# A first attention block's queries prepared among the last gates, and one ring of five tiles for two kinds of filler

## The chip, the cores and the metric

One core of one Trainium2 chip runs the whole program in one launch. The time is device microseconds of one execution; the kernel before took 1732.0 us, the median of three runs (1731.62 to 1733.96). A core has five engines with a queue each: TensorE (PE, matmuls and transposes), VectorE (DVE), ScalarE (ACT), GpSimd (POOL) and SyncE (SP), which here issues the DMAs. Each engine takes its instructions in a fixed order; a waiting instruction holds all that stand behind it.

## The reference

One inference step of a hybrid encoder on 1088 tokens (1024 of a prompt, 64 of a sample with 128 cached keys). Cut to what matters here:

```python
h = rmsnorm(x); p = h @ w_in          # columns of three branches and three gate blocks
qa, ka, va, qi, ki, wi, ub, qm, gates = split(p)
# branch A: per query, an indexer picks the best 256 admissible keys, then attention
score = einsum('bths,bth->bts', relu(einsum('bthd,bsd->bths', qi, ki)), wi)
_, sel = top_k(where(adm, score, -inf), topk)
out_a = softmax(q . k_sel) @ v_sel     # 8 query heads, 2 key heads, head_dim 64
# branch B: trailing means over 2, 4, 8, 16 frames, a linear map per group
# branch M: cross-attention into 256 memory tokens
merged = sum_b sigmoid(gate_b) * (branch_b @ w_o_b)
x += merged @ w_out; x += swiglu(rmsnorm(x))
```

The outputs are the new x and the new cache entries. Every product is made in float32 accuracy from values split into a high and a low part in a rounded format: three matmuls (high by high, low by high, high by low) for one.

## The kernel before

The tokens lie in nine blocks of 128 (the last has 64). The work goes in stages: projections of the branches; selection of the keys by a bisection on DVE and ACT (L835 to L893: counts of scores above a step, then a new step); attention over block after block with the unselected keys masked; output projection and the feed-forward part. While DVE and ACT are bound by the bisection, PE is given filler: the gates (`fill_gate`, L603, tiles named fsg, a tanh on ACT at L243, then a store), the products of the pooling branch (`fill_ob`, L609, tiles named fpt), and inside the attention the products of the memory branch (`fill_om`, L629, tiles named gt). Gates and products go through DRAM: a gate tile is stored; `fill_ob` loads a stored gate tile (L616), DVE multiplies it with the product (L619), and the result is stored into side_m (L620); `fill_om` loads two tiles of side_m (L626), DVE multiplies (L638), POOL adds (L639), and the sum is stored into side_a (L640). All three take their sums from the PSUM tile fl.

In the program's text 48 gate tiles come first, then 24 pooling tiles, later 24 more gate tiles. The gate tiles have a ring of two, the pooling tiles a ring of three: the load into a slot waits for the store out of it.

The attention goes over the blocks in the order 2, 0, 1, 3, 8, 4, 5, 6, 7. For each, `queries_t` (L928) loads the queries (q), splits them (ACT L936, DVE L937, tile qs), transposes eight heads on PE (L940) and copies the result on ACT (L942, tile qT). `softmax` makes the logits on PE (L961, PSUM tile tr), adds the mask and takes the extreme value on DVE (L965, mx), the exponential on ACT (L967), and the division on POOL (L969 a power, L971 a scaling). `values` transposes the probabilities (L984), splits them (ACT L987, DVE) and multiplies by the values (L991).

On POOL and DVE, in the stretch from 440 to 545 us, the head normalisation of projected rows also runs: POOL makes a reciprocal root (L125 a scaling, L126 a power, tile hr), DVE applies it (L216, tile qn) and rotates (L152 to L155) with the tables cosa and sina, which POOL scales after their load (L546, L547). L893 on DVE moves the scores by a rank in the bisection.

The order on each engine is not the program's text. The whole is traced in a context with a scheduler (`schedule_with_timeline_sim=True`) that plays the instructions through a simulated time and lets the one that is ready go; so a change at one place can alter the order on every engine around it.

Of the kernel before, what the change touches and what calls it, by code (L numbers as in the profile page):

```python
# [8 lines left out]
F32 = mybir.dt.float32  # L9
F32R = mybir.dt.float32r  # L10
AF = mybir.ActivationFunctionType
OP = mybir.AluOpType
# [17 lines left out]
HA, HDA = 8, 64  # L30
# [3 lines left out]
NP = NF // 2  # L34
NEG = -1e30
FPT, FSG = 3, 2
ACT_SEL = (3, 5, 7)
DVE_SEL = (8, 2, 4, 6)
INADM = -3.0e38
# [6 lines left out]
def encoder_step(ctx: ExitStack, tc: tile.TileContext, a: dict, o: list):  # L46
# [30 lines left out]
    def mm(dt=F32):  # L77
        return psum[0].tile([128, 512], dt, name="mm", tag="mm", bufs=n_mm[0])
# [126 lines left out]
    def raw_tile():  # L205
        return wp.tile([128, 1024], F32, name="raw", tag="raw", bufs=3)
# [32 lines left out]
    def fsig(w, c0, cn, low_last=False):  # L239
        ps = fps(cn)  # L240
        gate_block(w, hh[:, :, c0:c0 + cn], hl[:, :, c0:c0 + cn], ps, low_last)
        sg = fil.tile([128, 384], F32, name="fsg", tag="fsg", bufs=FSG)[:, :cn]
        A.activation(sg, ps, AF.Tanh, scale=0.5)  # L243
        return sg

# [4 lines left out]
    with tc.tile_pool(name="xphase", bufs=1) as xp:  # L250
# [11 lines left out]
        for c in (0, 512):  # L262
            ps = mm()
# [345 lines left out]
    def fill_ob():  # L609
        for f in range(KT):  # L610
            if f % 2 == 0:
                ow = wblock(a["w_ob"][f:f + 2].rearrange("f p k j -> p f k j"), (2, 4, 128), fraw())
            for c0, cn in CH:
                c1 = c0 + cn
                pt = fil.tile([128, 384], F32, name="fpt", tag="fpt", bufs=3)[:, :cn]
                SP.dma_start(pt, gate_b[f, :, c0:c1])  # L616
                ps = fps(cn)
                matmul3(ps, [(ow[0][:, f % 2, k], ow[1][:, f % 2, k], bh[:, k, c0:c1], bl[:, k, c0:c1]) for k in range(4)])
                V.scalar_tensor_tensor(pt, pt, 1.0, ps, op0=OP.add, op1=OP.mult)  # L619
                SP.dma_start(side_m[f, 1, :, c0:c1], pt)  # L620
# [177 lines left out]
    load_keys(0, 384)  # L798


    for b in range(2):
        V.memset(score[b], 0.0)
        V.memset(score[b][0:64, nkey[b] - 64:], -NEG)
# [109 lines left out]
    with tc.tile_pool(name="att", bufs=1, side="right") as ap_:  # L913
# [12 lines left out]
                lo_of(vb[:n, b0:b1, kv, 1], vs, vb[:n, b0:b1, kv, 0])  # L926

        def queries_t(b):  # L928
            t0, n = TS[b]
            q = ap_.tile([128, HA, HDA], F32, name="q", tag="q", bufs=2)  # L930
            ld = SP.dma_start(q[:n].rearrange("p h d -> p (h d)"), q_a[t0:t0 + n])
            if b in KEYS_AT:
                with tc.issue_after(ld.ins):
                    load_keys(*KEYS_AT[b])
            qs = ap_.tile([128, HA, 2, HDA], F32R, name="qs", tag="qs", bufs=1)
            A.copy(qs[:n, :, 0], q[:n])  # L936
            V.tensor_tensor(qs[:n, :, 1], q[:n], qs[:n, :, 0].bitcast(F32), op=OP.subtract)  # L937
            ps = tr(F32R)
            for h in range(HA):
                PE.transpose(ps[:, h * 128:h * 128 + n], qs[:n, h].rearrange("p s d -> p (s d)"), ident_r[:n, :n])  # L940
            qT = ap_.tile([128, HA, 128], F32R, name="qT", tag="qT", bufs=2)
            A.copy(qT[:, :, :n], ps.rearrange("p (h t) -> p h t", h=HA)[:, :, :n])  # L942
            return qT
# [64 lines left out]
                fill_om(*rest.pop(0))  # L1008
                n -= 1

        for b in (2,0,1,3,8,4,5,6,7):
            qT = queries_t(b)
            for kv in range(2):
                probs = softmax(b, kv, qT)
                if todo:
                    fill(todo[0] // 3 if todo[0] < 8 else 2)
                    values(*todo)
                todo = (b, kv, probs)
                fill(-1, 1)
        values(*todo)  # L1020
    kv2_c.__exit__(None, None, None)
    kv_c.__exit__(None, None, None)
    sel_c.__exit__(None, None, None)
    ps2_c.__exit__(None, None, None)
# [511 lines left out]
```

## Time and profile before

| | |
|---|---|
| median of three runs | 1732.0 us (1731.62 to 1733.96) |
| the profiled execution, its time | 1732.96 us |
| the profiled execution, its span | 1731.1 us |
| PE, DVE, ACT, POOL busy | 1692.6, 1172.7, 809.2, 418.6 us |
| mean granted clock of PE | 0.996 of full speed |

The span goes from the first to the last instruction, the time of an execution includes what lies around it. Busy times of the engines overlap. A granted clock of 1.00 is the full clock of PE; 0.5 would be half of it.

### The profile page before, as it was taken

What the parts mean: (1) busy time and instruction counts of PE and PEld (TensorE: products, weight loads), DVE (VectorE), ACT (ScalarE), POOL (GpSimd) and SP (SyncE); (2) the same over time, 40 slices, a digit from 0 to 9 for tenths busy, and PEclk for the clock granted to TensorE, in tenths of its full rate; (3) what the DMA queues carried; (4) which work ended last, traced back from release to release, by engine and by line L of the source; (5) the groups of instructions that cost most, each with busy time, mean ns of one, the idle gap of its engine ahead of it and who ended that gap; (6) DMA issues with size and microseconds to landing.
All of it is one profiled execution on the core that took longest, in us unless ns stands there. A gap on an engine that the chain in (4) does not pass through costs nothing.

```text
span 1731.1 us, 32521 instructions
## 1 busy us (share of the span) xinstructions
PE 1692.6 (98%) x12088; PEld 1640.9 (95%) x12088; DVE 1172.7 (68%) x2602; ACT 809.2 (47%) x1951; POOL 418.6 (24%) x474
## 2 busy tenths in 40 slices
PE   8999999999999999999899999999999999999999
PEld 7999999999899998877798999999999999999999
DVE  7566999999964443788874688656668556475553
ACT  5457577746532442569732344334334333353431
POOL 4201325355421122775302442001101000000000
PEclk9999999999999999999999999999999999999999
DMA  7121541233366325750273327442535443497761
GB/s 235 56 68 57 174 143 47 73 98 98 109 198 205 100 93 170 244 181 1 78 264 115 113 92 242 150 150 99 203 135 182 150 150 122 144 344 257 213 191 52
DMA packets 147262, 250.85 MB, mean 145 GB/s; under 512 B 16920, under 2 KB 93328, under 8 KB 147104
## 3 DMA queue, kind: packets, MB, share of 16 engines
q1 hardware_dynamic: 147104, 248.78, 43.8%
q8 instruction: 95, 1.56, 0.4%
q14 instruction: 63, 0.52, 0.1%
HBM read 173.63 MB, written 75.09 MB: 144 GB/s over the span
## 4 chain that ended last, share of the span: by engine, by line
PE 77%; DVE 9%; ACT 5%; issue 4%; DMA 3%; POOL 2%; SPq 0%; DVEq 0%; ACTq 0%; POOLq 0%
PE mm L1190 24%; PE mm L122 19%; PE fl L122 14%; PE mm L1417 13%; ACT junk_a L835 2%; PE acc L991 1%; DVE junk_v L838 1%; PE tr L961 1%; DVE wlo L86 1%; PE mm L984 1%; PE mm L379 1%; DVE pl L86 1%; DVE lo L86 1%; DMA side_m<-fpt 1%; DMA gt<-side_m 1%
## 5 line engine op out<-in xcount | busy, mean ns | idle before, releaser
L1190 PE MATMUL mm<-hi,whi 128*128 128x288 f32 (+1 forms) x1120 | 323.0, 289 | 2.3 <-ACT whi L1182 2.3
L1190 PE MATMUL mm<-hi,wlo 128*128 128x288 f32 (+1 forms) x1120 | 323.4, 290 | 0.1
L1190 PE MATMUL mm<-lo,whi 128*128 128x288 f32 (+1 forms) x1120 | 323.4, 289 | 0.0
L1190 PEld LDWEIGHTS mm<-hi,whi 128*128 128x128 f32 x1120 | 211.8, 189 | 3.0 <-ACT whi L1182 3.0
L1190 PEld LDWEIGHTS mm<-lo,whi 128*128 128x128 f32 x1120 | 211.7, 189 | 0.0
L1190 PEld LDWEIGHTS mm<-hi,wlo 128*128 128x128 f32 x1120 | 211.0, 189 | 0.4 <-DVE wlo L86 0.4
L122 PE MATMUL fl<-hh,whi 128*128 128x362 f32 (+1 forms) x576 | 189.9, 330 | 1.7 <-DVE fpt L619 1.0
L122 PE MATMUL fl<-hl,whi 128*128 128x362 f32 (+1 forms) x576 | 189.5, 329 | 0.1
L122 PE MATMUL fl<-hh,wlo 128*128 128x362 f32 (+1 forms) x576 | 188.0, 330 | 0.0
L1417 PE MATMUL mm<-ul,wh 128*128 128x256 f32 (+1 forms) x600 | 171.7, 288 | 0.0
L1417 PE MATMUL mm<-uh,wh 128*128 128x256 f32 (+1 forms) x600 | 171.2, 288 | 0.0
L1417 PE MATMUL mm<-uh,wl 128*128 128x256 f32 (+1 forms) x600 | 170.3, 288 | 0.0
L86 DVE TENSOR_TENSOR wlo<-raw,whi 128x1024 fp32r<-128x1024 f32 (+1 forms) x76 | 77.1, 1026 | 58.7 <-ACT whi L1182 38.6
L835 ACT ACTIVATE junk_a<-score,cand_a,sgn_a 128x512 f16<-128x512 f32 (+2 forms) x93 | 95.5, 1027 | 43.5 <-DVE cand_a L852 31.2
L1417 PEld LDWEIGHTS mm<-ul,wh 128*128 128x128 f32 x600 | 112.7, 188 | 0.0
L1417 PEld LDWEIGHTS mm<-uh,wh 128*128 128x128 f32 x600 | 112.4, 188 | 0.0
L1417 PEld LDWEIGHTS mm<-uh,wl 128*128 128x128 f32 x600 | 112.2, 188 | 0.0
L122 PEld LDWEIGHTS fl<-hh,whi 128*128 128x128 f32 x576 | 108.1, 188 | 3.0 <-POOL whi L96 1.2
L122 PEld LDWEIGHTS fl<-hl,whi 128*128 128x128 f32 x576 | 108.2, 188 | 0.9 <-DVE hl L86 0.4
L122 PEld LDWEIGHTS fl<-hh,wlo 128*128 128x128 f32 x576 | 108.0, 188 | 0.6
L86 DVE TENSOR_TENSOR wl<-raw,wh 128x512 fp32r<-128x512 f32 x75 | 51.7, 690 | 69.8 <-ACT wh L1407 69.8
L838 DVE TENSOR_SCALAR_CACHE_REDUCE junk_v<-score,cand_v 64x192 f16<-64x192 f32 (+1 forms) x124 | 93.9, 757 | 2.6
(410 smaller groups left out, 4669.7 us busy)
## 6 DMA issues: line engine op xcount, KB each, us to landing
uf<-u SPq DMA_DIRECT2D x75, 272.0 KB, 4.7
raw<-in_w_up_dram SPq DMA_DIRECT2D x26, 512.0 KB, 4.3
fraw<-in_w_gates_dram SPq DMA_DIRECT2D x23, 512.0 KB, 3.9
fr<-in_w_gate_dram SPq DMA_DIRECT2D x22, 512.0 KB, 4.3
dr<-in_w_down_dram SPq DMA_DIRECT2D x22, 512.0 KB, 5.7
s<-dr SPq DMA_DIRECT2D x22, 512.0 KB, 3.1
raw<-s SPq DMA_DIRECT2D x44, 256.0 KB, 3.8
side<-side_a SPq DMA_DIRECT2D x8, 1088.0 KB, 6.1
```

Of the source, the lines that this page charges most:

```text
L86: return V.tensor_tensor(lo, src, hi.bitcast(F32), op=OP.subtract)
L122: PE.matmul(ps, l, r, start=i == 0, stop=i == len(prods) - 1)
L379: PE.matmul(ps[:n, :cn], qt[:, h, :n], kstack[:, k0 + c:k0 + c + cn], start=True, stop=True)
L835: A.activation(junk[:n, :nk], sc, AF.Sign, bias=bj, scale=1.0 if scale is None else scale[:n, j:j + 1], accum_out=sj)
L838: V.tensor_scalar(junk[:n, :nk], sc, bj, None, op0=OP.is_ge, op1=OP.add, accum_out=sj)
L961: PE.matmul(lg[:n, i * 512:i * 512 + cn], qT[:, h, :n], kT[:, kv, s, k0 + c:k0 + c + cn], start=s == 0, stop=s == 1)
L984: PE.transpose(pt[:cn, i * n:(i + 1) * n], probs[i][:, c:c + cn], ident[:n, :n])
L991: PE.matmul(acc, vv, r, start=ji == 0 and i == 0, stop=ji == nj - 1 and i == 1)
L1190: PE.matmul(dst[i], l, r, start=start and j == 0, stop=stop and j == 11, skip_group_check=True)
L1417: PE.matmul(acc[f, i], l[:, fs], r[:, cs], start=start and j == 0, stop=stop and j == 2, skip_group_check=True)
```

## The change

The first block of the attention (block 2) has its queries loaded into a borrowed weight tile (`raw`), split and transposed right behind the first load of keys, in the program's text before attention's pools are opened and so, for the scheduler, free to run beside the last gates. The split is made a function that both places call. The transposes use two PSUM tiles of 512 columns (mm) in place of one of 1024 (tr), so the copy on ACT is in two halves, and the result lies in a small pool of its own that stays open to the end of the attention. Gate tiles and pooling tiles take one ring of five.

```diff
-        sg = fil.tile([128, 384], F32, name="fsg", tag="fsg", bufs=FSG)[:, :cn]
+        sg = fil.tile([128, 384], F32, name="fsg", tag="fsg", bufs=FSG + FPT)[:, :cn]
...
-                pt = fil.tile([128, 384], F32, name="fpt", tag="fpt", bufs=3)[:, :cn]
+                pt = fil.tile([128, 384], F32, name="fpt", tag="fsg", bufs=FSG + FPT)[:, :cn]
...
     load_keys(0, 384)
+    def split_queries(qs, q, n):
+        A.copy(qs[:n, :, 0], q[:n])
+        V.tensor_tensor(qs[:n, :, 1], q[:n], qs[:n, :, 0].bitcast(F32), op=OP.subtract)
+
+    early_c = tc.tile_pool(name="early", bufs=1)
+    early = early_c.__enter__()
+    qT_first = early.tile([128, HA, 128], F32R, name="qT0")
+    q0 = raw_tile()[:, :512].rearrange("p (h d) -> p h d", h=HA)
+    SP.dma_start(q0.rearrange("p h d -> p (h d)"), q_a[TS[BLOCKS[0]][0]:TS[BLOCKS[0]][0] + 128])
+    qs0 = early.tile([128, HA, 2, HDA], F32R, name="qs0")
+    split_queries(qs0, q0, 128)
+    for g in (0, 4):
+        ps = mm(F32R)
+        for h in range(4):
+            PE.transpose(ps[:, h * 128:h * 128 + 128], qs0[:, g + h].rearrange("p s d -> p (s d)"), ident_r)
+        A.copy(qT_first[:, g:g + 4], ps.rearrange("p (h t) -> p h t", h=4))
...
         def queries_t(b):
+            if b == BLOCKS[0]:
+                return qT_first
...
-            A.copy(qs[:n, :, 0], q[:n])
-            V.tensor_tensor(qs[:n, :, 1], q[:n], qs[:n, :, 0].bitcast(F32), op=OP.subtract)
+            split_queries(qs, q, n)
...
-        for b in (2,0,1,3,8,4,5,6,7):
+        for b in BLOCKS:
```

The new lines shift the numbers: L126 of before is L127 after, L546 is L547, L619 is L620; from the inserted lines on the shift is 19 or 20 (L893 is L912, L940 is L960, L961 is L981, L984 is L1004).

The scheduler's order changes at places that the diff doesn't name. The first is on POOL between the weights' rounding and the next blocks' normalisation, at about 464 to 470 us of the profile; hr is the reciprocal root, cosa and sina are the rotary tables. Before:

```order
L125 TENSOR_SCALAR hr<-hss 64x4
L126 TENSOR_TENSOR hr<-hr,mhalf 64x4
L125 TENSOR_SCALAR hr<-hss 128x2
L546 TENSOR_TENSOR cosa<-cosa,g_3763 128x576
L126 TENSOR_TENSOR hr<-hr,mhalf 128x2
L547 TENSOR_TENSOR sina<-sina,g_3764 128x576
L125 TENSOR_SCALAR hr<-hss 128x2
L126 TENSOR_TENSOR hr<-hr,mhalf 128x2
```

After:

```order
L126 TENSOR_SCALAR hr<-hss 64x4
L127 TENSOR_TENSOR hr<-hr,mhalf 64x4
L126 TENSOR_SCALAR hr<-hss 128x2
L127 TENSOR_TENSOR hr<-hr,mhalf 128x2
L547 TENSOR_TENSOR cosa<-cosa,g_3763 128x576
L126 TENSOR_SCALAR hr<-hss 128x2
L548 TENSOR_TENSOR sina<-sina,g_3764 128x576
L127 TENSOR_TENSOR hr<-hr,mhalf 128x2
```

The power that follows the scaling of the third block has moved from behind the table cosa to in front of it; sina now stands between a scaling and its power.

The second is DVE at the same place: fpt is the pooling product, got and rank the end of a bisection step, score the index scores, qn the normalised rows, rope the rotation. Before:

```order
L619 SCALAR_TENSOR_TENSOR fpt<-fpt,fl 128x362
L890 TENSOR_TENSOR got_a<-ssum_a,cut_a 128x3
L890 TENSOR_TENSOR got_v<-ssum_v,cut_v 128x4
L891 SCALAR_TENSOR_TENSOR rank_a<-got_a,rank_a 128x3
L891 SCALAR_TENSOR_TENSOR rank_v<-got_v,rank_v 128x4
L216 TENSOR_TENSOR qn<-mm,hr 128x128
L893 TENSOR_SCALAR score_95<-score_95,rank_a 128x512
L893 TENSOR_SCALAR score_97<-score_97,rank_a 128x768
L893 TENSOR_SCALAR score_99<-score_99,rank_a 128x1024
L888 TENSOR_SCALAR step_v<-rank_v 128x4
L152 TENSOR_TENSOR rope_3815<-qn,cosa 128x128
L619 SCALAR_TENSOR_TENSOR fpt<-fpt,fl 128x362
```

After:

```order
L620 SCALAR_TENSOR_TENSOR fpt<-fpt,fl 128x362
L217 TENSOR_TENSOR qn<-mm,hr 128x128
L909 TENSOR_TENSOR got_a<-ssum_a,cut_a 128x3
L909 TENSOR_TENSOR got_v<-ssum_v,cut_v 128x4
L910 SCALAR_TENSOR_TENSOR rank_a<-got_a,rank_a 128x3
L910 SCALAR_TENSOR_TENSOR rank_v<-got_v,rank_v 128x4
L912 TENSOR_SCALAR score_95<-score_95,rank_a 128x512
L912 TENSOR_SCALAR score_97<-score_97,rank_a 128x768
L912 TENSOR_SCALAR score_99<-score_99,rank_a 128x1024
L620 SCALAR_TENSOR_TENSOR fpt<-fpt,fl 128x362
L907 TENSOR_SCALAR step_v<-rank_v 128x4
L153 TENSOR_TENSOR rope_3815<-qn,cosa 128x128
```

The normalisation (qn) has moved in front of the bisection's bookkeeping, and the second pooling product stands directly behind the three score updates, no longer behind a step and a rotation.

The third is PE in the first attention block, from the end of an output product (fl) to the next one; tr with kT, qT are logits, tr with ident_r the transposes of a later block's queries, mm with ident the transposes of the probabilities (pr). Before:

```order
L122 MATMUL fl<-bl,whi 128x384
L122 MATMUL fl<-bh,wlo 128x384
L940 MATMUL tr<-ident_r,qs 128x128 x8
L961 MATMUL tr<-kT,qT 128x384 x2
L984 MATMUL mm<-ident,pr 128x128 x8
L122 MATMUL fl<-bh,whi 128x384
```

After:

```order
L123 MATMUL fl<-bl,whi 128x384
L123 MATMUL fl<-bh,wlo 128x384
L981 MATMUL tr<-kT,qT_7700 128x384 x8
L960 MATMUL tr<-ident_r,qs 128x128 x8
L1004 MATMUL mm<-ident,pr 128x128 x2
L981 MATMUL tr<-kT,qT_7700 128x384 x2
L1004 MATMUL mm<-ident,pr 128x128 x6
L981 MATMUL tr<-kT,qT 128x128 x4
L123 MATMUL fl<-bh,whi 128x384
```

Before, the product that ends at the first rows (the seventh of the memory branch) precedes the transposes of the probabilities; after, the sixth does, and the seventh begins behind the eight transposes and four logits of the next block. The eight new transposes (L816) stand earlier, in front of the twelve matmuls of the second product of the memory branch, which the rows don't show.

## Rows read from the trace of the kernel before

**Rows 1.** The page: its first line, and section 1 (engine, busy us, share, instructions).
```profile
span 1731.1 us, 32521 instructions
...
PE 1692.6 (98%) x12088; PEld 1640.9 (95%) x12088; DVE 1172.7 (68%) x2602; ACT 809.2 (47%) x1951; POOL 418.6 (24%) x474
```

**Rows 2.** The waits of PE over the whole span, two of its rows (times, longest).
```profile
PE fl L122 <- DVE fpt L619: 4.3, 2, 3.2
PE fl L122 <- DVE gt L638: 3.2, 7, 0.8
```

**Rows 3.** Busy time by stretch (the first row names the columns).
```profile
core 0: us, PE busy (x) PEld busy (x) DVE busy (x) ACT busy (x) POOL busy (x), PEclk, DMA share, GB/s
...
460.00:480.00 20.00, 16.75 (x106) 16.43 (x105) 17.50 (x54) 5.65 (x19) 6.19 (x7) 0.91 0.67 205
...
676.00:690.00 14.00, 10.95 (x63) 10.13 (x64) 9.13 (x20) 4.15 (x13) 8.17 (x7) 1.00 0.88 298
690.00:704.00 14.00, 12.34 (x57) 11.25 (x56) 6.88 (x21) 6.78 (x19) 7.22 (x9) 0.76 0.90 327
...
780.00:800.00 20.00, 18.24 (x119) 15.31 (x117) 17.82 (x43) 18.58 (x44) 12.69 (x15) 1.00 0.00 1
```

**Rows 4.** Timeline of POOL at 466 us (start, duration, instruction, idle before).
```profile
466.07 1.43 POOL L546 TENSOR_TENSOR cosa<-cosa,g 128x576 f32<-128x576 f32 x1 [2.20 <-DMA cosa<-in_cos_a_dram]
467.46 0.71 POOL L126 TENSOR_TENSOR hr<-hr,mhalf 128x2 f32<-128x2 f32 x1
```

**Rows 5.** Timeline of DVE, 464 to 472 us.
```profile
464.93 0.53 DVE L619 SCALAR_TENSOR_TENSOR fpt<-fpt,fl 128x362 f32<-128x362 f32 x1
...
468.19 0.29 DVE L216 TENSOR_TENSOR qn<-mm,hr 128x128 f32<-128x128 f32 x1 [2.39 <-POOL hr L126]
468.40 2.61 DVE L893 TENSOR_SCALAR score<-score,rank_a 128x512 f32<-128x512 f32 x3
...
471.20 0.52 DVE L619 SCALAR_TENSOR_TENSOR fpt<-fpt,fl 128x362 f32<-128x362 f32 x1
```

**Rows 6.** The chain of waits, 460 to 480 us (start, us, what).
```profile
461.78 4.15 DMA cosa<-in_cos_a_dram
...
471.78 5.49 PE fl L122 x23
```

**Rows 7.** The chain of waits, 515 to 545 us: products at full rate.
```profile
515.00 5.80 PE fl L122 x35
```

**Rows 8.** Timeline of DVE at 536 us, a pooling tile that waited.
```profile
536.11 0.53 DVE L619 SCALAR_TENSOR_TENSOR fpt<-fpt,fl 128x364 f32<-128x364 f32 x1 [4.96 <-DMA fpt<-gate_b]
```

**Rows 9.** The tile fpt: who waited for its loads, and its DMAs.
```profile
  DVE fpt L619: 11.0, 4
...
DMA to landing us min/median/max: 1.8/2.7/6.7
```

**Rows 10.** Timeline of PE, 686 to 702 us, without the pieces of the output products.
```profile
686.24 0.87 PE L940 MATMUL tr<-ident_r,qs 128*128 128x128 f32 x8 [1.11 <-DVE qs L937]
688.22 0.97 PE L961 MATMUL tr<-kT,qT 128*128 128x384 f32 x4 [1.10 <-ACT qT L942]
...
702.08 1.04 PE L984 MATMUL mm<-ident,pr 128*128 128x128 f32 x8
```

**Rows 11.** Timeline of DVE, 688 to 697 us.
```profile
688.90 0.56 DVE L638 SCALAR_TENSOR_TENSOR gt<-gt,fl 128x384 f32<-128x384 f32 x1 [0.76 <-PE tr L961]
...
695.90 0.55 DVE L965 CUSTOM_DVE_ANT_0 pr<-tr,score 128x384 f32<-128x384 f32 x1
```

**Rows 12.** The chain of waits, 672 to 705 us.
```profile
682.78 5.99 DMA gt<-side_m
...
689.51 3.85 PE fl L122 x12
```

**Rows 13.** Timeline of POOL, 698 to 702 us.
```profile
698.28 1.01 POOL L639 TENSOR_TENSOR gt<-gt 128x384 f32<-128x384 f32 x1
699.27 2.27 POOL L971 TENSOR_SCALAR pr<-pr,sm 128x384 f32<-128x384 f32 x4
```

More of the change, by code (lines that the diff above doesn't have):

```diff
@@ L36 @@
 FPT, FSG = 3, 2
+BLOCKS = (2, 0, 1, 3, 8, 4, 5, 6, 7)
 ACT_SEL = (3, 5, 7)
@@ L1021, in encoder_step @@
     kv2_c.__exit__(None, None, None)
+    early_c.__exit__(None, None, None)
     kv_c.__exit__(None, None, None)
```

## The prediction

> **What bounds the kernel now.** I read the page first: PE is busy 1692.6 of 1731.1 us, VectorE (DVE) 68%, ScalarE (ACT) 47%, GpSimd (POOL) 24% [rows 1]. So the time is TensorE's work plus 38.5 us in which it stands still, plus what a lowered clock costs. A change that adds no matmul can move only the last two. The waits of PE say which of its neighbours are late; two rows lie in stretches that the change touches: products behind fpt (the pooling tiles), 4.3 us in two waits, one of them 3.2, and products behind gt (the merge tiles), 3.2 us in seven [rows 2]. The table by stretch then shows where the clock drops: granted 0.91 in 460 to 480 us and 0.76 in 690 to 704, while 676 to 690 is at 1.00 with PE busy 10.95 of 14 us [rows 3]. The two levels are 1.2 and 2.4 GHz. Of the first, 471.78 us, PE had waited over 3 us just before; of the second no single wait was above 1.11 us [rows 10], PE had simply been idle often.
>
> **Part one, the wait at 471 us, which the edit doesn't name.** The new instructions make the scheduler order POOL anew: before, the power for one block's normalisation (L126) stands behind the cosine table's product (L546); after, in front of it. Before, POOL waits 2.20 us for the cosine table, whose DMA took 4.15 us, runs L546 from 466.07, and does the power at 467.46 [rows 4, 6]. DVE, in order, stands 2.39 us at L216 for that power, until 468.19, then does three index updates (L893, 2.61 us), and only then the pooling product L619 at 471.20, for which PE waits until 471.78 [rows 5, 6]. DVE was ready at 468.19 - 2.39 = 465.80. After the change the power is done by then, and the next L619 stands directly behind the index updates: 465.80 + 0.29 + 2.61 = 468.7, plus 0.52, and PE starts near 469.2 instead of 471.78, 2.6 us earlier. PE then ran 23 products in 5.49 us; the same kind at full rate took 5.80 us for 35, 0.166 each [rows 6, 7], so 23 need 3.8, and 1.7 us of lowered clock may go too, since only about 0.6 us of idle time is left before them. Upper end 4.3. Lower end 2.4, DVE's own wait, since DVE is busy 17.5 of 20 us in that stretch [rows 3] and PE meets it again for the rotary work and the key copies behind. Nothing at all if DVE is held by the table elsewhere; that is a rival below. I take 3.7 us, near the upper end, because the clock row is the firmer of the two.
>
> **Part two, one ring of five.** Each pooling tile is loaded, multiplied on DVE and stored; its slot comes free when the store lands. With three tiles the cycle is 2.7 + 0.53 + 2.7 = 5.9 us by the median landing [rows 8, 9], while PE eats three tiles in 3 x 12 x 0.166 = 6.0 us [rows 7]. So every landing above the median makes DVE wait: 11.0 us in four cases, the longest 4.96 at 536.11 [rows 8, 9]. With five tiles the cover is 10.0 us; even one landing at the maximum, 2.7 + 0.53 + 6.7 = 9.9, fits [rows 9]. But PE has products of its own to do while DVE waits: it paid only 4.3 - 3.2 = 1.1 us [rows 2]. I take 1.0; the ends are 0 and 1.3 (a little for the transfers queued behind such a load on SP). What the ring gives up: before, three pooling loads lay ready from the start; now the first ones wait for a gate tile's store. The gates end before the pooling products begin, and a landing (2.7) is shorter than the 10.0 us between a slot's uses, so I put this at nothing. Where it is not covered, everything behind the waiting load on SP is late; that is the slower rival.
>
> **Part three, the first block's queries.** What moves: one query load on SP, an ACT copy, a DVE subtraction, eight transposes (0.87 us [rows 10]) and the copy of their result, now in two halves on ACT, so one ACT instruction more. The transposes go into PE's wait before the first output products; the ACT and DVE instructions go among the last gates, where both have slack [rows 1]. The load borrows one of three weight tiles, which can hold an output weight back; less than a microsecond, I count nothing. What goes: the 1.11 us wait for the split and the 1.10 us wait for the transposed copy [rows 10]. What is late next: five of the output-product blocks before attention need side tiles, and the load for the fifth (issued 682.78, landing 5.99 us later) releases DVE's L638 at 688.90, which releases the next block at 689.51 [rows 11, 12]. The change does not touch that load. So PE idles until about 689.0 in any case, and the block of 12 that follows may run at half clock as before (3.85 us [rows 12]; at full rate 12 x 0.166 = 2.0 [rows 7]).
> The gain is that by then DVE has had the logits of three heads, so behind that block only the fourth is missing. Before, the fourth head's maximum began at 695.90 [rows 11], and the eight transposes of its probabilities ended at 702.08 + 1.04 = 703.12 [rows 10]: 7.2 us. After, the block ends at 689.0 + 3.85 = 692.9, the maximum can begin at 693.4, and with 7.2 us behind it they end at 700.6 at worst; POOL's 2.27 us for four heads [rows 13] is in that chain, the 1.01 us that POOL spent there on a merge [rows 13] need not be, so 699.6. With the block at full rate it would be 1.85 us earlier, 697.7, and about 696.6 if the 2.0 us block that PE did inside the old chain (the new order puts it behind) held part of it up. That is 3.5 to 6.5 us ahead, less this block still to be done: 1.5 to 4.5. I take 3.0. The later blocks are reshuffled too, in a stage where PE, DVE and ACT are all busy above 17.8 of 20 us [rows 3]; I count nothing and widen the range by 3 us each way.
>
> The Trainium skill, "TensorE: Matmul & The Clock Gate", section "HAM oscillation — how this bites in real kernels", ties the lowered clock to one long wait for data. The trace agrees at 471.78 and does not at 690, where the clock is 0.76 after waits of 1.11 us at most [rows 3, 10]. By that rule the longer wait that this change leaves before 689 would be what lowers the clock, and part three would stay at its low end, 1.5, the sum 6.2; by the row it is lowered with or without it.
>
> **The sum.** 3.7 + 1.0 + 3.0 = 7.7 us. The profiled execution took 1732.96 us (span 1731.1 [rows 1], 1.86 outside it), so 1725.3; the median of the three runs is 0.96 lower, so 1724.3 us. A measurement of this kernel can tell about 0.2%, 3.5 us, from no change: faster is below 1728.5, slower above 1735.5.
>
> **Rivals.** (1) Attention's start keeps its end: the merge load at 682.78 decides, the clock falls as deep, and the early logits only wait. For it: that load is untouched [rows 12]. Against: PE waited seven times for DVE's merge products [rows 2], and DVE has less to do there. Then 1732.0 - 4.7 = 1727.3.
> (2) The wait at 471 us only moves, and attention's later reshuffling takes back its gain. For it: DVE's load of 17.5 in 20 us; the table's landing is the same [rows 3, 6]. Against: the pooling product stands ahead of the rotary work that needs the table. Only the ring is left: 1731.0.
> (3) Slower: the shared ring puts a wait into SP's queue, in front of weights and key tiles. For it: a store took up to 6.7 us to land [rows 9], and SP serves in order. Against: the 10.0 us cover. If each of the 24 pooling loads held SP so that PE lost 0.5 us, that is 12 us in place of the gain of 1.0: 1732.0 - 6.7 + 12 = 1737.3. It decides from 6.7/24 = 0.28 us a load, and is told from no change from 0.43.
>
> **How the numbers follow.** Forecast 0.60, its own range 1719 to 1728 (terms at 10.1 and 4, with 3 us more for the reshuffling on the fast side); rival one 0.18, rival two 0.14, rival three 0.08. Faster: 0.60 + 0.18 less 0.03 for the upper tails = 0.75; same 0.14 + 0.03 = 0.17; slower 0.08. The range 1718 to 1731 holds the forecast, rival one and most of rival two.
>
> **What would show it.** Part one: DVE's wait for the power near 466 gone, PE resuming near 469 and the clock of 460 to 480 at 1.00. Part two: no DVE wait over 1 us for fpt. Part three: transposes before the first output products, the first maximum before 687, probabilities transposed by 700, and PE still idle before 689 on gt. Wrong it is if PE's total idle time doesn't fall by some 4 us, if SP shows pooling loads waiting for stores with PE behind them, or if 700 to 866 us takes longer than it did.

## The result, and the profile after

The changed kernel took 1723.95 us, the median of six runs (1723.24 to 1727.91), beside 1732.32 us for the kernel before on the same chip: a ratio of 0.995, 95% interval [0.994, 0.9961], some 8.4 us. The forecast was 1724.3. Profiled, its span is 1721.9 us in an execution of 1723.64.

The page of the changed kernel, its first line and section 1, which answers to [rows 1]:

```profile
span 1721.9 us, 32518 instructions
...
PE 1687.8 (98%) x12088; PEld 1636.3 (95%) x12088; DVE 1176.3 (68%) x2602; ACT 811.1 (47%) x1952; POOL 422.4 (25%) x474
```

PE does the same 12088 matmuls in 4.8 us less busy time. As no matmul went, that is clock (13.6 us of half clock in the first trace, 3.4 in the second, and half of the difference is 5.1); its idle time fell by 38.5 - 34.1 = 4.4 us. The table by stretch (columns as in [rows 3]) says where the clock rose: 0.91 to 1.00 at 460 to 480 us and 0.76 to 0.88 at 690 to 704.

```profile
460.00:480.00 20.00, 18.85 (x133) 18.35 (x132) 18.80 (x56) 6.11 (x23) 5.73 (x7) 1.00 0.80 238
520.00:540.00 20.00, 20.00 (x125) 19.56 (x125) 7.99 (x13) 3.10 (x7) 2.09 (x2) 1.00 0.92 279
676.00:690.00 14.00, 11.17 (x62) 10.21 (x61) 9.95 (x23) 4.75 (x17) 7.60 (x6) 1.00 0.99 319
690.00:704.00 14.00, 12.34 (x72) 11.07 (x71) 8.08 (x24) 7.56 (x21) 10.90 (x14) 0.88 0.83 282
```

**At 471 us.** DVE's timeline in the changed kernel (start, duration, instruction, idle before), to be held against [rows 5]:

```profile
467.08 0.53 DVE L620 SCALAR_TENSOR_TENSOR fpt<-fpt,fl 128x362 f32<-128x362 f32 x1
467.52 0.28 DVE L217 TENSOR_TENSOR qn<-mm,hr 128x128 f32<-128x128 f32 x1
...
468.11 1.68 DVE L912 TENSOR_SCALAR score<-score,rank_a 128x512 f32<-128x512 f32 x3
469.70 0.53 DVE L620 SCALAR_TENSOR_TENSOR fpt<-fpt,fl 128x362 f32<-128x362 f32 x1
470.14 1.27 DVE L907 TENSOR_SCALAR step_v<-rank_v 128x4 f32<-128x4 f32 x1
...
473.32 0.23 DVE L154 TENSOR_TENSOR rope<-qn,sina 128x64 f32<-128x64 f32 x1 [1.16 <-POOL sina L548]
```

The 2.39 us wait is gone and the second pooling product follows the first by 2.6 us where it took 6.3. PE doesn't wait there at all. DVE waits 1.16 us later, for the sine table, and PE meets that as the forecast's lower end had it, at the key copies:

```profile
475.59 0.28 PE L572 MATMUL mm<-ident_r,kd 128*128 128x128 f32 x1 [1.10 <-ACT kd L565]
```

**The pooling products.** Two rows of the changed kernel: DVE's one long wait for a pooling tile, and the tile's summary for those who wait (us, times), beside [rows 8, 9]:

```profile
536.32 0.53 DVE L620 SCALAR_TENSOR_TENSOR fpt<-fpt,fl 128x362 f32<-128x362 f32 x1 [3.65 <-DMA fpt<-gate_b]
```
```profile
  DVE fpt L620: 5.2, 2
```

5.2 us of waits in place of 11.0, and none of them reaches PE.

**The start of attention.** PE's timeline in the changed kernel, beside [rows 10]: the early transposes, the logits, and the waits between them.

```profile
673.24 0.80 PE L816 MATMUL mm<-ident_r,qs 128*128 128x128 f32 x8
674.86 0.44 PE L123 MATMUL fl<-bh,whi 128*128 128x384 f32 x1 [0.82 <-ACT qT L817]
...
681.22 0.85 PE L981 MATMUL tr<-kT,qT 128*128 128x384 f32 x4
...
683.88 0.45 PE L123 MATMUL fl<-bh,wlo 128*128 128x384 f32 x1 [1.46 <-DVE wlo L87]
...
687.88 0.44 PE L123 MATMUL fl<-bh,whi 128*128 128x384 f32 x1 [0.98 <-DVE gt L639]
...
693.68 1.21 PE L960 MATMUL tr<-ident_r,qs 128*128 128x128 f32 x8 [1.00 <-DVE mx L985]
...
695.91 1.46 PE L1004 MATMUL mm<-ident,pr 128*128 128x128 f32 x6
```

And DVE's first maximum, with what DVE does behind it:

```profile
685.68 0.54 DVE L985 CUSTOM_DVE_ANT_0 pr<-tr,score 128x384 f32<-128x384 f32 x1
...
686.15 1.21 DVE L87 TENSOR_TENSOR wlo<-raw,whi 128x1024 fp32r<-128x1024 f32 x1
687.29 0.54 DVE L639 SCALAR_TENSOR_TENSOR gt<-gt,fl 128x384 f32<-128x384 f32 x1
```

The logits come 7.0 us earlier than the 688.22 of [rows 10], the first maximum at 685.68, the probabilities are transposed by 697.4 (703.12 before), and in front of the sixth product PE waits for gt until 687.88: the order of events is the forecast's. But PE reached this stage 2.3 us earlier than before (its 4450th matmul starts at 666.82 in place of 669.16), which the forecast's times don't contain. Counted from there the logits are 4.7 us ahead and the probabilities 3.4, and the product behind gt begins 0.7 us later than before. Nor was it the load of gt that held this product, as the forecast had it: the load had landed 0.8 us before DVE multiplied, and the multiplication (L639) stands without idle time behind the split of an output weight (wlo). The product then ran at full clock, not at half, and a new wait of 1.46 us, for the low half of an output weight, stands in the fifth.

**Stage by stage.** Both kernels issue the same number of matmuls, so the start of the k-th one can be compared where the orders agree. From the traces, us from one such matmul to another, and in brackets the us of half clock in it; the last column is the stretch around the wait of 1.8 us at the end of attention, which no kernel here touches. In the two kernels with six matmuls more the count is shifted by six. The labels are those of the experiments below.

| kernel | 0 to 3000 | 3000 to 3450 (449 to 516 us) | 3450 to 3750 (516 to 565) | 4450 to 5250 (669 to 817) | 5400 to 5550 (845 to 874) |
|---|---|---|---|---|---|
| before | 446.85 | 67.25 (3.4) | 48.57 | 148.20 (6.8) | 28.92 (3.4) |
| before, again (e7) | 448.22 | 69.18 (6.8) | 50.08 | 146.96 (6.8) | 27.42 |
| changed | 448.76 | 64.12 | 47.22 | 142.75 (3.4) | 27.41 |
| changed, again (e0) | 446.16 | 63.91 | 46.87 | 142.98 | 27.42 |
| ring alone (e1) | 446.21 | 63.75 | 48.65 | 149.69 (13.7) | 27.39 |
| queries alone (e2) | 447.94 | 68.93 (6.8) | 48.55 | 143.46 | 28.90 (3.4) |
| power first (e3) | 446.87 | 65.60 | 51.62 (3.4) | 147.03 (6.8) | 27.41 |
| ring, table first (e4) | 446.93 | 64.93 | 48.08 | 147.13 (3.4) | 28.92 (3.4) |
| ring of four (e5) | 446.57 | 65.03 | 47.51 | 145.14 (3.4) | 27.46 |
| keys later (e6) | 448.86 | 64.34 | 48.14 | 148.52 (6.8) | 28.87 (3.4) |
| idle matmuls (e8) | 447.99 | 68.90 (6.8) | 49.65 | 145.52 | 28.90 (3.4) |
| ring, idle matmuls (e9) | 447.35 | 64.08 | 46.93 | 146.16 (3.4) | 28.91 (3.4) |
| values later (e10) | 447.62 | 63.84 | 47.87 | 146.73 (10.2) | 28.93 (3.4) |

The first pair of traces alone gives 3.1, 1.4, 5.4 and 1.5 us gained in the last four columns and 1.9 lost in the first. The other rows tell which of that stays.

The fourth of these columns can be split. At the 4570th matmul (697.8 us in the kernel before, 693.7 in the changed one), and again at the 5040th, the old and the new order have issued the same matmuls. Averages of the five profiles with the old order (before, e7, e1, e3, e4) and the four with the new one (changed, e0, e2, e5), in us, as PE's busy and idle time:

| order | 4450 to 4570 | 4570 to 5040 | 5040 to 5250 |
|---|---|---|---|
| old | 29.0 (24.0 busy, 4.9 idle) | 80.4 (75.4, 5.1) | 38.4 |
| new | 26.9 (21.6 busy, 5.4 idle) | 78.0 (74.4, 3.6) | 38.7 |

So at the start of attention PE waits no less than before; what is gained there, 2.0 us, is clock. The other 2.5 us are gained in the blocks behind the first.

### The profile page after: what moved, and what is told of

Its sections match the earlier page's. It is cut to its first block, busy times and chain, and to the rows that moved or that the text cites. A ratio compares the mean times of both kernels' runs of the same rounds, so it can differ in the third digit from the quotient of the medians.

```text
span 1721.9 us, 32518 instructions
## 1 busy us (share of the span) xinstructions
PE 1687.8 (98%) x12088; PEld 1636.3 (95%) x12088; DVE 1176.3 (68%) x2602; ACT 811.1 (47%) x1952; POOL 422.4 (25%) x474
## 4 chain that ended last, share of the span: by engine, by line
PE 64%; DVE 5%; issue 2%; ACT 2%; POOL 2%; DMA 1%; SPq 0%; POOLq 0%; DVEq 0%; ACTq 0%
PE mm L1211 24%; PE mm L1438 13%; PE mm L123 13%; PE fl L123 8%; PE acc L1011 1%; PE tr L981 1%; DVE lo L87 1%; PE mm L1004 1%; DMA gt<-side_m 1%; ACT pr L987 1%; DVE wlo L87 1%; DVE pl L87 0%; DVE pr L985 0%; PE mm L674 0%; POOL gt L640 0%
## 5 line engine op out<-in xcount | busy, mean ns | idle before, releaser
L87 DVE TENSOR_TENSOR wlo<-raw,whi 128x1024 fp32r<-128x1024 f32 (+1 forms) x76 | 76.8, 1022 | 57.7 <-ACT whi L1203 38.4
```

The source lines that it names most:

```text
L87: return V.tensor_tensor(lo, src, hi.bitcast(F32), op=OP.subtract)
```

## The experiments

Where a time is given, it is a median with its ratio to the kernel before, run in turn on the same chip.

**e1, the ring alone.**

```diff
-        sg = fil.tile([128, 384], F32, name="fsg", tag="fsg", bufs=FSG)[:, :cn]
+        sg = fil.tile([128, 384], F32, name="fsg", tag="fsg", bufs=FSG + FPT)[:, :cn]
...
-                pt = fil.tile([128, 384], F32, name="fpt", tag="fpt", bufs=3)[:, :cn]
+                pt = fil.tile([128, 384], F32, name="fpt", tag="fsg", bufs=FSG + FPT)[:, :cn]
```

> The ring of five alone, with the queries as before. Theory (the three stretches add up; the wait at 471 us belongs to the ring, since the ring moves the orders up to 545 us and the queries those from 673 us on): PE reaches 545 us about 4.5 us earlier than before (3.1 at 454 to 490 us, 1.4 behind it), the attention's start is as before, with granted clock below 1.00 in 690 to 704; time 1727 to 1728.5. Rival (the stretches depend on each other, or the 2.1 us that the changed kernel lost ahead of 454 us is the ring's own cost): only 2 to 2.5 us gained, 1729.5 to 1730.5, and PE late by 1 to 2 us at 300 us.

1726.65 us, 0.9965 [0.9953, 0.9977]: about 6 us, a little more than the theory's 3.5 to 5; in the traces PE is 3.8 us ahead at 565 us. The wait at 471 us is gone with the ring alone, and the new places in POOL's and DVE's order are there with it. On each engine this kernel and the changed one have the same order until the early queries' own instructions come in (SP at 615 us, ACT at 654, DVE at 655, PE at 673). The start of attention is not as before but has 13.7 us of half clock.

**e2, the early queries alone.**

```diff
-        sg = fil.tile([128, 384], F32, name="fsg", tag="fsg", bufs=FSG + FPT)[:, :cn]
+        sg = fil.tile([128, 384], F32, name="fsg", tag="fsg", bufs=FSG)[:, :cn]
...
-                pt = fil.tile([128, 384], F32, name="fpt", tag="fsg", bufs=FSG + FPT)[:, :cn]
+                pt = fil.tile([128, 384], F32, name="fpt", tag="fpt", bufs=FPT)[:, :cn]
```

(against the changed kernel)

> The early queries alone, with rings of two and three. Theory: nothing changes up to 670 us, the wait of 3.2 us at 471 us and the lowered clock behind it stay; from 673 to 866 us 5.4 us are gained as in the changed kernel, and the lowered clock at 867 us goes: 1725.5 to 1727. Rival (attention's start only pays since the ring shifted the clock's phase): 3 us or less, 1729 to 1730, and the clock is lowered at 867 us as before.

1728.53 us, 0.9977 [0.9968, 0.9986]: 4.0 us, between the two. The attention stage is that of the changed kernel (143.46), the stretch at 449 to 516 us that of before, and worse: a wait of 3.68 us and 6.8 us of half clock. At the end of attention the lowered clock came back, against the theory. The two halves give 6.1 + 4.0 = 10.1 us where the whole gives 8.4 to 9: they add up within their intervals.

**e0, the changed kernel again** (no edit).

> The changed kernel itself again, to see which part of its trace comes back. Theory (the 2.1 us that it lost ahead of 454 us are chance waits on landings): that loss is not the same again, and the waits at 188 and 310 us are absent or elsewhere; the gains in the three stretches are within 0.5 us of the first trace; time 1723 to 1726. Rival (the loss belongs to the kernel): PE is again 2 us late at 454 us.

1722.99 us, 0.9948 [0.9934, 0.9961]. The 1.9 us lost ahead of 449 us are not there (446.16): they were chance. So is what the first pair showed at 845 to 874 us: over the thirteen profiles half clock follows the wait of 1.8 us in seven and not in six, with the same order on every engine.

**e3, the power first.**

```diff
+            if b == 0:
+                with tc.issue_after(last_pow[0].ins):
+                    scaled()
```

(cut to the lines that move the order; scaled() makes the two products of the tables, issue_after puts them behind the power in POOL's order)

> Kernel before, rings as before, with only the power of the first key block forced in front of the cosine and sine tables on POOL. Theory (what the ring brings at 471 us is POOL's order, not the tiles): DVE's 2.39 us wait for the power goes, but its rotation, which needs the table, now stands ahead of the score updates, so PE's wait of 3.2 us at 471 us shrinks to about 2: time 1729 to 1731. Rival (the ring's tiles themselves removed the wait): PE's wait stays over 3 us, 1732 to 1733.

1733.76 us, 1.0006 [0.9996, 1.0017]: no gain, as the rival had it in time, though not in cause. With the rings as before and the power in front of the cosine table on POOL, as in the changed kernel, PE still waited 3.56 us. PE's row of that wait, and DVE's timeline, which shows why:

```profile
471.51 0.43 PE L122 MATMUL fl<-bh,whi 128*128 128x362 f32 x1 [3.56 <-DVE fpt L629]
```
```profile
464.87 0.28 DVE L218 TENSOR_TENSOR qn<-mm,hr 128x128 f32<-128x128 f32 x1
...
467.95 1.47 DVE L152 TENSOR_TENSOR rope<-qn,cosa 128x128 f32<-128x128 f32 x1 [2.46 <-POOL cosa L549]
469.34 1.67 DVE L903 TENSOR_SCALAR score<-score,rank_a 128x512 f32<-128x512 f32 x3
470.94 0.52 DVE L629 SCALAR_TENSOR_TENSOR fpt<-fpt,fl 128x362 f32<-128x362 f32 x1
```

The power is early, but the scheduler has put the rotation, which needs the table itself, ahead of the score updates and the pooling product. The wait of 2.46 us only changed its name. The theory's 2 us for PE was too low, in part since the rotation took 1.47 us beside POOL's table product.

**e4, the ring with the table first.** The ring of e1, and the power forced behind the cosine table, as before:

```diff
+        with tc.issue_after(behind.ins) if behind else nullcontext():
+            return G.tensor_tensor(r, r, mhalf[:r.shape[0], :r.shape[1]], op=OP.pow)
```

(cut; behind is the product of the cosine table, and only the first key block's normalisation hands it over)

> The ring of five alone, and the power of the first key block forced behind the cosine table on POOL, as it stood before. DVE's order has shifted with it: the score updates and the pooling product now stand ahead of the normalisation that needs the power. Theory (after the last runs: what removes the wait at 471 us is that DVE has the pooling product ahead of everything that waits for the table, not where POOL has the power): PE's wait at 471 us is gone although POOL's order is that of before, 3 to 3.5 us gained at 454 to 490 us, time within 1 us of the ring alone. Rival (the power's place on POOL is what counts): PE waits again over 2 us near 471 and the time is 1729.5 or more.

1726.57 us, 0.9969 [0.9956, 0.9981], level with e1. DVE's timeline, and the two waits of PE for fpt:

```profile
465.89 1.68 DVE L896 TENSOR_SCALAR score<-score,rank_a 128x512 f32<-128x512 f32 x3
...
467.55 0.52 DVE L622 SCALAR_TENSOR_TENSOR fpt<-fpt,fl 128x362 f32<-128x362 f32 x1
469.84 0.29 DVE L217 TENSOR_TENSOR qn<-mm,hr 128x128 f32<-128x128 f32 x1 [1.77 <-POOL hr L127]
```
```profile
471.05 0.41 PE L122 MATMUL fl<-bh,whi 128*128 128x364 f32 x1 [0.39 <-DVE fpt L622]
...
474.88 0.43 PE L122 MATMUL fl<-bh,whi 128*128 128x362 f32 x1 [1.59 <-DVE fpt L622]
```

DVE waits 1.77 us for the late power, but with the pooling product behind it already done; PE waits 0.39 us there, and 1.59 us at 474.88. So it is DVE's order that pays at 471 us: the pooling product ahead of everything that hangs on the table. Where POOL has the power decides little (64.93 against 63.75 us in that stretch).

**e5, a ring of four.**

```diff
-        sg = fil.tile([128, 384], F32, name="fsg", tag="fsg", bufs=FSG + FPT)[:, :cn]
+        sg = fil.tile([128, 384], F32, name="fsg", tag="fsg", bufs=4)[:, :cn]
...
-                pt = fil.tile([128, 384], F32, name="fpt", tag="fsg", bufs=FSG + FPT)[:, :cn]
+                pt = fil.tile([128, 384], F32, name="fpt", tag="fsg", bufs=4)[:, :cn]
```

> The changed kernel with a shared ring of four tiles in place of five. POOL's order is that of the changed kernel; on DVE the rotation that needs the table stands behind the first of three score updates, ahead of the pooling product. Theory (DVE's order decides at 471 us, the number of tiles at 520 to 545): PE waits 2 us or more near 471 again, and fpt waits of DVE come back in part, 0.5 to 1 us of PE; with a lowered clock behind the wait 3 to 5 us slower than the changed kernel, 1727 to 1729. Rival (four tiles do as well as five and the order is indifferent): within 1 us of the changed kernel.

1724.16 us, 0.9949 [0.9936, 0.9963]. The mechanism came, the size didn't: DVE again waits for the table ahead of the pooling product, PE waits 1.88 us at 470.3, and the stretch takes 65.03 us instead of 64; but no half clock followed, and four tiles do as well as five at 516 to 565 us (47.51). In time the rival holds: the ratio is that of the changed kernel (0.995 and 0.9948). The rows of DVE, and PE's wait:

```profile
468.97 0.29 DVE L153 TENSOR_TENSOR rope<-qn,cosa 128x128 f32<-128x128 f32 x1 [2.65 <-POOL cosa L547]
...
469.71 0.53 DVE L620 SCALAR_TENSOR_TENSOR fpt<-fpt,fl 128x362 f32<-128x362 f32 x1
```
```profile
470.29 0.43 PE L123 MATMUL fl<-bh,whi 128*128 128x362 f32 x1 [1.88 <-DVE fpt L620]
```

**e6, keys later.**

```diff
-    KEYS_AT = {0: (384, 768), 3: (768, SEQ + PAST + DEC)}
+    KEYS_AT = {3: (384, 768), 8: (768, SEQ + PAST + DEC)}
```

> The changed kernel, the second and third load of keys each bound to a later block (blocks 3 and 8 in place of 0 and 3), so that 0.9 MB less is loaded in 676 to 690 us. Theory (attention's start is now held by landings of the output weights and of gt, which share the DMA engines with these keys): the waits for wlo (1.46 us) and gt (0.98) shrink, 1 to 2.5 us faster than the changed kernel, 1721 to 1723. Rival (the same bytes are only in the way later): no change at the end of attention, within 0.7 us of the changed kernel.

1728.78 us, 0.9979 [0.9967, 0.999], where the changed kernel has 0.995: some 5 us slower, so the theory fell. With the DMA engines' share at 682 to 688 us down from 0.97 to 0.72, the waits at attention's start hardly moved (1.26 for wlo, 0.98 for gt). They were not waits for landings: DVE is busy for all of those 6 us in both kernels, and the split of wlo and the product gt stand in its queue. The stage, reordered by the scheduler, lost 5.5 us beside e0, 4.2 of them in waits of PE.

**e7, the kernel before again** (no edit).

> The kernel before itself, a second profile. Theory (which short stretches of lowered clock occur is chance in this kernel, the order of the engines is not): PE's wait of over 3 us at 471 us and the waits of attention's start come back within 0.3 us; the stretches of lowered clock at 690 to 704 and at 867 us need not. Rival: both come back alike, so a clock of 1.00 at 867 us in the changed kernel is its own merit.

One run, 1735.18 us. The waits came back (4.07 us at 474, 1.11 and 1.10 at attention's start), the half clock at 690 to 704 too, that at 867 us didn't. The wait at 474 was 0.8 us longer than the first trace's, above the 0.3 that the theory allowed, and 6.8 us of half clock followed it in place of 3.4.

**e8, idle matmuls.** The kernel before, and behind the eight transposes of the first block (cut; last_t is the last of these):

```diff
+            if b == 2:
+                idle = tr()
+                with tc.issue_after(last_t.ins):
+                    for _ in range(6):
+                        PE.matmul(idle[:, :384], ident_r, kT[:, 0, 0, :384], start=True, stop=True)
```

> The kernel before with six matmuls whose result nobody reads, put on PE behind the transposes of the first block's queries, where it otherwise waits 1.10 us for their copy; all orders are else those of before. Theory (over the same 801 matmuls from 666 to 817 us the old order takes 147 to 150 us with PE busy 134 to 137, the new one 143 to 145 with 131 to 133: most of what the early queries bring is a clock that stays up, not shorter waits): no or one stretch of half clock in 690 to 704 in place of two, the stretch 145 to 146.5 us, time 1.5 to 3 us below before. Rival (waits decide; the clock falls for other reasons): the half-clock stretches stay, the time is that of before within 1 us.

1734.04 us, 1.001 [0.9998, 1.0021]. In the profile the half clock at attention's start is gone and the stage is 1.4 to 2.7 us shorter than in the two profiles of before; in the time nothing is gained. The mean granted clock of the twelve runs, 0.9977, is above the 0.9971 of the runs of before beside it, 1 us worth, and the six matmuls are 1 us of PE. So PE's waits can be filled; why the time doesn't follow, no run shows.

**e9, the ring with the same idle matmuls** (the diffs of e1 and e8 together).

> The ring of five with the same six idle matmuls, no early queries. Theory: as the ring alone, 1726.6, less 1.5 to 3 us of clock: 1723.5 to 1725, within 2 us of the changed kernel. Rival: as the ring alone within 1 us.

1726.69 us, 0.9964 [0.995, 0.9977]: as the ring alone, which was the rival, though the mean clock rose from 0.9980 to 0.9990. In the profiles e8 and e9 take 27.15 and 27.26 us for what is 4450 to 4570 in the table above, nearly as little as the new order, but 79.97 and 80.52 for 4570 to 5040, as the old one does. Keeping PE busy in these waits doesn't replace the early queries.

**e10, the values later.** The changed kernel, with the load and the split of the values traced behind the first half of the first block's logits (cut; load_values() holds both):

```diff
                 probs = softmax(b, kv, qT)
+                if not todo:
+                    load_values()
```

> The changed kernel with the load and the split of the values moved in the program's text behind the first half of the first block's logits, so that SP's queue has the output weights, the store of gt and the queries first, and DVE does its 4 us of value splits after the first maxima and not before. Theory (in the changed kernel the first maxima, at 685.7 us, and the weights' wait of 1.5 us are held by that work): first maximum 3 us earlier, wait for wlo under 0.5 us, the 801 matmuls of 667 to 810 us in 140 to 142 us in place of 143, time 1721 to 1722.5. Rival (the values come late for the first products with them, or the reordered attention loses more, as with the later keys): PE waits over 1 us for vb or pl at 695 to 705, 145 us or more, time 1725 or more.

1725.48 us, 0.996 [0.9946, 0.9974], some 2 us slower than the changed kernel by the ratios, which their intervals don't tell apart; the time is the rival's. The first maximum came 4.6 us earlier than in the changed kernel (3.8 counted from the stage's start) and the wait for wlo went, as the theory had it:

```profile
681.04 0.55 DVE L986 CUSTOM_DVE_ANT_0 pr<-tr,score 128x384 f32<-128x384 f32 x1
```

But the stage took 146.73 us. The same 801 matmuls in five kernels, before, changed, e2, e8 (with six more) and e10, each from its own table by stretch (stretch, its length, busy time of PE, PEld, DVE, ACT, POOL, clock, DMA share, GB/s):

```profile
669.16:817.37 148.21, 135.02 (x802) 117.59 (x802) 111.89 (x256) 91.39 (x230) 92.69 (x108) 0.98 0.50 160
```
```profile
666.82:809.57 142.75, 131.99 (x801) 116.03 (x801) 112.93 (x255) 91.64 (x230) 95.68 (x108) 0.99 0.52 164
```
```profile
671.92:815.38 143.46, 131.34 (x802) 114.62 (x802) 112.67 (x255) 91.43 (x230) 95.51 (x108) 1.00 0.52 163
```
```profile
673.25:818.77 145.52, 133.28 (x808) 115.41 (x808) 112.58 (x256) 91.49 (x230) 92.74 (x108) 1.00 0.50 163
```
```profile
665.97:812.70 146.73, 134.62 (x801) 118.13 (x801) 113.97 (x255) 90.86 (x230) 90.46 (x108) 0.97 0.50 160
```

Length less busy time is what PE waited: 13.2, 10.8, 12.1, 12.2 and 12.1 us. The busy time is nearly all clock: 131.3 where it is 1.00, up to 135 where it is lower; of e8's 133.3 at 1.00 the six matmuls are 1.0, and 1 us is not accounted for. In e10 what was gained at the start was waited for later, and 10.2 us of half clock took the rest. No version tried beats the changed kernel.

## Why the prediction was right, and where not

The sum was 7.7 us and the time moved 8.4 (9 by the ratio of e0); but its terms don't all stand as they were written. All three came out larger than I took them (4.6, 1.6 and 4.2 us, averaged over the profiles), and add up to 10.4, more than was timed. That the sum came so near is in part luck. Of the signs of being wrong that I had named none came: PE's idle time fell by 4.4 us, and the blocks behind the first took 2.5 us less.

**Part one, 3.7 us.** The pair of traces gives 3.1; the four profiles with the old order there (before, e7, e2, e8) average 68.6 us, four with the ring of five and the changed kernel's order (changed, e0, e1, e9) 64.0: 4.6 us, a little above the upper end of 4.3, since the lowered clock lasted 6.8 us in three of the four and 3.4 in the one I read. The step "the scheduler orders POOL anew" was named as the cause; e3 and e4 show it isn't. The cause is the place of the pooling product on DVE, which I had also shown but as a consequence. The working (465.80 + 0.29 + 2.61) survived because it used DVE's order. Its 2.61 for the score updates was too long: in the changed kernel, with POOL at rest, they took 1.68.

**Part two, 1.0 us.** 1.35 in the pair, between nothing and 3.2 for other pairs, 1.6 on average (49.2 for before, e7, e2, e8; 47.6 for changed, e0, e1, e9, e6, e10). Right in kind: the shared ring costs nothing that these traces show. In this stretch PE waited 1.0, 2.1, 0, 0.8 and 3.1 us for fpt with three tiles (before, e7, e2, e8, e3), and not at all with five or four; the term was read from one execution and taken too low. That DVE would have no wait over 1 us was wrong (3.65). The step that failed is the cover of 10.0 us with one long landing: the store that freed this slot was issued at 526.29 and the load behind it at 531.25, and both took 4.9 us to land. The slower rival, SP held by loads, did not come: PE waited up to 1.3 us for a load of q_m with five tiles (e1), but up to 1.1 with three (e8).

**Part three, 3.0 us.** Mis-sized: 5.4 in the pair, and over the profiles with the old order (148.20, 146.96, 149.69, 147.03, 147.13, mean 147.8) and the new (142.75, 142.98, 143.46, 145.14, mean 143.6) 4.2. Three steps failed. The product behind the wait for gt did not run "at half clock as before". And I took the gain for waits: over these profiles the length less PE's busy time is 12.8 us on average with the old order and 11.7 with the new, 1.1 us, while the busy time of the same matmuls went from 135.0 to 131.9, 3.1 us, nearly all of it clock. In the timed runs of e2 the clock is the smaller part: 0.9979 against 0.9970 beside it, 1.6 of 4.0 us. The third step is the later blocks, counted at nothing: of the 4.2 us they bring 2.5, 1.5 of these in waits. In the first block the waits of 1.11 and 1.10 us went, but 0.82, 1.46 and 0.98 came in their place. No run has early queries with the old order of the later blocks, so what the queries themselves bring there and what the new order does is not shown. That the order can matter by as much as the whole term, e6 shows, with 4.2 us more of waits than e0; what e10 loses beside e0, 3.7 us, is nearly all clock.

**The clock.** The mean granted clock over all timed runs is 0.9969 for before (67 runs) and 0.9991 for the changed kernel (12). That is 0.0022 of 1730 us, 3.8 us: a good 40% of the gain. I had 1.7 us for it, all of it at 471 us. The Trainium skill, "TensorE: Matmul & The Clock Gate", section "HAM oscillation — how this bites in real kernels", ties the lowered clock to a long wait for data. These runs agree only in part: waits of 3.6 to 4.1 us at 471 us were followed by 6.8 us of half clock in three profiles, one of 3.25 by 3.4 us, but e3's of 3.56 by none, while e3's next, of 3.06 at 537 us, was followed by 3.4 us; and the wait of 1.8 us after attention by half clock in seven of thirteen. What decides there stays open. So does why idle matmuls (e8) raise the clock in the profile and leave the time.

**The rivals.** The first (attention's start keeps its end) is excluded in time by e2, 4.0 us with the queries alone; that the early logits would only wait is what PE's idle time in the first block did show. The second named the right danger, since DVE does meet the table again (1.16 us at 473.32), but PE pays 1.1 us for it and not 3.

## What to carry to other kernels

When a scheduler orders by simulated time, read the new order for every engine before and after, and test a suspected mover by forcing that one place, reading again what else moved with it: here the visible move on POOL was harmless and the one on DVE paid. A single profile is one draw: stretches of half clock and late landings moved single stages by 1 to 3 us between executions of one kernel, so size a term by two profiles or by the mean clock of many runs. A wait that goes from the start of a stage that is bound by several engines is worth what is left at the stage's end, not what left its start.

## What the runs showed of the hardware

DVE's instructions took longer while POOL ran its product of a 128x576 table beside them. The three score updates took 2.61 us in the kernel before [rows 5] and 2.60 in e2, but 1.68 in the changed kernel and in e4, where POOL stood still during them. In the kernel before POOL ran in that stretch:

```profile
468.12 1.42 POOL L547 TENSOR_TENSOR sina<-sina,g 128x576 f32<-128x576 f32 x1
...
469.95 1.10 POOL L126 TENSOR_TENSOR hr<-hr,mhalf 128x2 f32<-128x2 f32 x1
```

A short instruction of POOL's did not do it: in e3 the same updates took 1.67 us, from 469.34, beside these:

```profile
469.36 0.19 POOL L125 TENSOR_SCALAR hr<-hss 128x2 f32<-128x2 f32 x1
469.63 0.76 POOL L126 TENSOR_TENSOR hr<-hr,mhalf 128x2 f32<-128x2 f32 x1
```

In the changed kernel the update of a 128x4 tile, 0.16 us elsewhere, took 1.27 us from 470.14, while POOL ran its cosine product:

```profile
469.96 1.43 POOL L547 TENSOR_TENSOR cosa<-cosa,g 128x576 f32<-128x576 f32 x1 [3.14 <-DVE score L912]
```

And e3's rotation took 1.47 us beside the sine table's product, where the same instruction took 0.28 in the kernel before.

The Trainium skill, "GPSIMD Engine Reference", section "1. Specifications", says that the two share their SBUF interfaces and contend for some kinds of DVE instruction. These rows agree for DVE, with 0.9 to 1.2 us as the price of one such meeting; whether the score updates, which read one large tile, are of the kinds that the page names, no run here shows.
